# Bounding the adding write-back of a 64-expert layer to the token rows

## The chip, the cores and the metric

The kernel runs on one core of one Trainium2 chip. The metric is the time on the device of one execution, in microseconds (us). A core has five engines with instruction queues of their own (TensorE "PE", VectorE "DVE", ScalarE "ACT", GpSimd "POOL", SyncE "SP") and 16 DMA engines that move data between the on-chip memory and DRAM for all of them.

## The reference

Two transformer-like blocks in float32, one sequence of 512 tokens of width 1024. What matters here is the mixture of 64 experts at the end of the second block: each token chooses 8 experts, each expert (a gated two-layer network with hidden width 256) is applied to its tokens, and the weighted results are added up by token.

```
def routed_experts(t, top_i, top_w, w_gu, w_dn):          # t (512, 1024), top_i (512, 8)
    ...
    padded = (counts + EXPERT_BLOCK - 1) // EXPERT_BLOCK * EXPERT_BLOCK      # EXPERT_BLOCK = 128
    ...
    rows = jnp.full((P,), T, jnp.int32).at[dest].set(tok_sorted)            # empty slots name row T
    wts = jnp.zeros((P,), jnp.float32).at[dest].set(w_flat[order])
    ...
    ys = lax.map(one_block, (rows.reshape(n_blk, EXPERT_BLOCK), blk_expert)).reshape(P, D)
    out = jnp.zeros((T + 1, D), jnp.float32).at[rows].add(ys * wts[:, None])
    return out[:T]
```

512 tokens with 8 experts each are 4096 pairs of a token and an expert. Evaluating the reference's router on its inputs gives the tokens of each expert: between 1 (expert 35) and 139 (expert 36), 64 on average. 17 experts have at most 32 tokens, 19 have between 33 and 74, and 28 have 76 or more. From expert 36 to 43 all eight have 74 or more; of experts 34 to 59, nine have at most 32. Expert 63 has 101. Expert 36 is the only one with more than 128; its 11 tokens over that make up the extra block named below.

## The kernel before

The kernel is one program: a delta-rule mixer, a mixture of 32 experts, a convolution mixer, a second mixture, a sparse-attention mixer, and last the class Moe64, the stage of 64 experts that this study is about. It works through 65 blocks of CAP = 128 slots: one for each expert, and one extra block (EXTRA = 1) for the tokens that did not fit into 128 slots. A block has as many occupied slots as its expert has tokens, and its occupied slots are the first ones. So 65 x 128 = 8320 slots hold 4096 pairs, and 4224 slots are empty.

For each block there are these steps, in the methods of Moe64:

- `fetch` (four blocks ahead, AHEAD = 4) makes the lists of row numbers on VectorE: `idx` (L2431), the token of each slot, and `dst` (L2432), the row to which the slot's result goes. For an empty slot `idx` is 4096, and `dst` is 512 plus the slot's number, a spare row of its own. Then it gathers the tokens' rows from DRAM with an indirect DMA from GpSimd (L2435), which has a bound on the row number (`bounds_check=T - 1`, with T = 512) and raises no error outside of it.
- `turn` and `up` (L2448, L2458 to L2460, with the helper `parts`, L537 and L538, which splits weights into two parts on ScalarE and VectorE), `turn_hid` (L2476) and `down` (L2487 and L2489) are the matrix products of the expert. TensorE does `turn_hid` once for each block.
- `spread` (L2494) adds the 128 rows of the block's result into the DRAM tensor `sum` with an indirect DMA from GpSimd. `sum` has T + 128 = 640 rows: 512 of tokens, and 128 spare ones.

Each `spread` waits for the one before it to have landed, since both add into `sum`. The buffers of `dst` turn over six deep, so VectorE writes the `dst` of block e + 4 into the buffer that block e - 2 used, and waits for the write-back of block e - 2 to have landed. The weights (three transfers of 1 MB for each expert) come on SyncE's queue (L244) into a ring of buffers; each transfer is issued when its buffer has been used up. At the end of the loop the two last write-backs follow one another, then the 512 token rows of `sum` are loaded (L2579), normalised and written out.

Of the kernel before, what the change touches and what calls it, by code (L numbers as in the profile page):

```python
# [13 lines left out]
OP = mybir.AluOpType  # L14
# [6 lines left out]
T = 512  # L21
# [1197 lines left out]
class HierMoe:  # L1219
# [248 lines left out]
    def spread(self, oh, rows):  # L1468

        K, nc = self.K, self.nc  # L1470
        ps = K.ps(BF16)
        for i in range(4):
            nc.tensor.transpose(ps[:rows, P * i:P * i + P], oh[:, i], K.identb)
        o = K.r.rot("oht", [P, T], 2)
        nc.scalar.activation(o[:rows], ps[:rows], AF.Copy)
        return o[:rows]
# [751 lines left out]
class Moe64:  # L2228
# [263 lines left out]
    def spread(self, y, dst):  # L2492

        self.nc.gpsimd.indirect_dma_start(out=self.sum[:], out_offset=bass.IndirectOffsetOnAxis(ap=dst[:, :1], axis=0),  # L2494
                                          in_=y, in_offset=None, compute_op=OP.add)

    def run(self, xT, gain, shift, gate, last):

# [212 lines left out]
```

## Time and profile before

| | us |
|---|---|
| median of 3 runs | 3480.29 |
| lowest and highest of the runs | 3479.04 and 3489.0 |
| the profiled execution: its time | 3479.72 |
| the profiled execution: its span, first to last instruction | 3478.0 |
| TensorE busy | 3170.4 (91% of the span) |
| the expert stage, from its first write-back to the end | 2745 to 3478 |

The span leaves out 1.7 us that lie around the profiled instructions. Busy time on TensorE is modelled from pipelined matmuls, so it shows where TensorE pauses rather than how near its peak it is.

### The profile page before, as it was taken

The page shows a single profiled execution, that of the slowest core. Times are in us where ns is not written, and L with a number is a line of the kernel's source. Part 1 is how long each engine was busy: PE and PEld are TensorE (multiplying, and loading weights), DVE is VectorE, ACT ScalarE, POOL GpSimd, SP SyncE. Part 2 cuts the span into 40 slices and gives each one's busy share as a digit, 9 for nine tenths or more (in the row PEclk, how much of TensorE's full clock was granted, in tenths as well). Part 3 has the DMA queues.
Part 4 walks back from the last instruction along what each step waited for, and adds up shares of the span by engine and source line. Part 5 has one row for each costly group of instructions (what it writes and reads, how often), then busy time and mean ns, then how long its engine had stood idle before and what let it go on. Part 6 is the DMA issues. An engine that isn't in the chain of part 4 may idle for free. (4 is left out here: it accounts for less than half of the span.)

```text
span 3478.0 us, 45287 instructions
## 1 busy us (share of the span) xinstructions
PE 3170.4 (91%) x16888; PEld 1926.0 (55%) x16888; DVE 1818.4 (52%) x4124; ACT 1450.0 (42%) x2730; POOL 606.8 (17%) x687
## 2 busy tenths in 40 slices
PE   7989999888998988997999989699999899999996
PEld 4667676663333333874333333488557566666663
DVE  3567764463333334444333333565463877776675
ACT  5544763541111112332111111363454476777774
POOL 3444423300000001001000001221101122222221
PEclk9989987999999999998999999898999999999998
DMA  5211212448999996245999999212315799999996
GB/s 198 109 67 46 101 55 85 146 165 351 419 419 399 378 397 264 99 171 207 420 420 396 366 382 403 86 61 97 134 64 194 258 331 351 364 365 366 351 351 190
DMA packets 144002, 871.92 MB, mean 251 GB/s; under 512 B 26273, under 2 KB 26785, under 8 KB 49953
## 3 DMA queue, kind: packets, MB, share of 16 engines
q1 hardware_dynamic: 103824, 748.73, 53.8%
q0 software_dynamic: 35568, 109.10, 11.2%
q10 hardware_dynamic: 4384, 11.14, 0.9%
q8 instruction: 135, 2.21, 0.3%
q14 instruction: 91, 0.74, 0.1%
HBM read 844.23 MB, written 57.67 MB: 259 GB/s over the span
## 5 line engine op out<-in xcount | busy, mean ns | idle before, releaser
L1439 PE MATMUL ps<-arena 128*64 128x512 f32 x1984 | 605.8, 615 | 2.6 <-DVE arena L1484 0.3
L537 ACT ACTIVATE phase<-arena 128x512 fp32r<-128x512 f32 (+1 forms) x729 | 447.9, 618 | 356.8 <-PE ps L550 204.7
L538 DVE TENSOR_TENSOR phase<-arena,phase 128x512 fp32r<-128x512 f32 (+1 forms) x663 | 433.8, 680 | 122.6 <-ACT phase L537 118.6
L550 PE MATMUL ps<-phase 128*128 128x512 f32 (+3 forms) x1000 | 395.6, 396 | 2.8 <-POOL phase L538 2.4
L1461 PE MATMUL ps<-arena 128*64 128x512 f32 x1040 | 353.0, 617 | 33.4 <-DVE arena L1451 33.4
L1439 PEld LDWEIGHTS ps<-arena 128*64 128x64 f32 x1984 | 174.7, 142 | 297.1 <-issue 287.1
L1441 ACT ACTIVATE phase<-ps 64x512 f32<-64x512 f32 x68 | 40.0, 588 | 695.5 <-PE ps L1439 695.5
L549 PE MATMUL ps<-phase 128*128 128x512 f32 (+1 forms) x736 | 282.6, 385 | 27.1 <-DVE arena L1764 16.6
L551 PE MATMUL ps<-phase 128*128 128x512 f32 (+1 forms) x736 | 279.4, 381 | 0.9 <-POOL phase L538 0.9
L2487 PE MATMUL ps<-arena 128*128 128x512 f32 x520 | 249.8, 604 | 2.6 <-ACT arena L2478 0.8
L538 POOL TENSOR_TENSOR phase<-arena,phase 128x256 fp32r<-128x256 f32 (+1 forms) x194 | 173.7, 897 | 370.2 <-ACT phase L537 313.7
L2460 PE MATMUL ps<-phase 128*128 128x512 f32 x520 | 228.2, 439 | 0.0
L550 PEld LDWEIGHTS ps<-phase 128*128 128x128 f32 (+2 forms) x1000 | 193.4, 193 | 39.2 <-POOL phase L538 3.3
L2458 PE MATMUL ps<-phase 128*128 128x512 f32 x520 | 212.3, 408 | 2.4 <-ACT phase L537 0.5
L2459 PE MATMUL ps<-phase 128*128 128x512 f32 x520 | 206.2, 396 | 6.6 <-DVE phase L538 6.5
L1406 POOL DMA_INDIRECT phase<-hrows,phase x34 | 33.8, 995 | 952.4 <-DVE phase L1442 472.2
L1442 DVE TENSOR_TENSOR phase<-ps,phase 64x512 f32<-64x512 f32 x68 | 47.2, 695 | 289.0 <-ACT phase L1441 287.8
L1461 PEld LDWEIGHTS ps<-arena 128*64 128x64 f32 x1040 | 95.7, 139 | 174.5 <-issue 134.9
L1484 DVE SCALAR_TENSOR_TENSOR arena<-ps,arena 128x512 f32<-128x512 f32 x272 | 185.2, 745 | 11.2 <-PE ps L1483 10.1
L2494 POOL DMA_INDIRECT sum<-arena x65 | 104.5, 1607 | 489.9 <-ACT phase L537 179.8
L1465 ACT ACTIVATE phase<-ps,phase 64x512 fp32r<-64x512 f32 x136 | 92.8, 683 | 196.1 <-PE ps L1461 170.0
L549 PEld LDWEIGHTS ps<-phase 128*128 128x128 f32 x736 | 140.1, 190 | 61.4 <-issue 24.8
(630 smaller groups left out, 5710.6 us busy)
## 6 DMA issues: line engine op xcount, KB each, us to landing
arena<-in_moe SPq DMA_DIRECT2D x548, 1024.0 KB
arena<-in_ada SPq DMA_DIRECT2D x72, 1024.0 KB
phase<-in_moe SPq DMA_DIRECT2D x28, 1024.0 KB
arena<-in_wina SPq DMA_DIRECT2D x16, 1024.0 KB
arena<-in_win SPq DMA_DIRECT2D x13, 1024.0 KB
arena<-in_winb SPq DMA_DIRECT2D x12, 1024.0 KB
arena<-in_wouta SPq DMA_DIRECT2D x4, 1024.0 KB
hrows<-arena POOLq DMA_DIRECT2D x8, 512.0 KB
```

Source lines behind the costliest of these rows:

```text
L537: self.nc.scalar.activation(h, x, AF.Copy)
L538: (eng or self.nc.vector).tensor_tensor(l, x, h, op=OP.subtract)
L549: mm(ps, w[0], x[0], start=start, stop=False)
L550: mm(ps, w[0], x[1], start=False, stop=False)
L551: mm(ps, w[1], x[0], start=False, stop=stop)
L1439: nc.tensor.matmul(ph[64 * j:64 * j + 64, :], x[:, k, :], u, start=k == 0, stop=k == 7)
L1461: nc.tensor.matmul(py[64 * j:64 * j + 64, :], hT[:, k, :], u, start=k == 0, stop=k == 3)
L1484: nc.vector.scalar_tensor_tensor(xT[:, f, :], ps, gate[:, f:f + 1], xT[:, f, :], op0=OP.mult, op1=OP.add)
L2458: nc.tensor.matmul(ps, x[0], h, start=start, stop=False)
L2459: nc.tensor.matmul(ps, x[0], l, start=False, stop=False)
L2460: nc.tensor.matmul(ps, x[1], h, start=False, stop=stop)
L2487: nc.tensor.matmul(py, hid[:, P * k:P * k + P], unit[:, 1024 * k + 512 * half:1024 * k + 512 * half + 512], start=k == 0, stop=k == 1)
```

## The change

The write-back gets the bound that the gather has: rows with numbers over 511 are left out of the transfer. The lists `dst` stay as they are, so it is the empty slots that are left out. They carried zero weight and went to the spare rows, which nothing reads.

```
     def spread(self, y, dst):
 
         self.nc.gpsimd.indirect_dma_start(out=self.sum[:], out_offset=bass.IndirectOffsetOnAxis(ap=dst[:, :1], axis=0),
-                                          in_=y, in_offset=None, compute_op=OP.add)
+                                          in_=y, in_offset=None, bounds_check=T - 1, oob_is_err=False, compute_op=OP.add)
```

The order of the instructions on all five engines is the same before and after.

## Rows read from the trace of the kernel before

**Rows 1.** Busy time by stretch of the stage; (x) counts instructions, columns named above.

```profile
core 0: us, PE busy (x) PEld busy (x) DVE busy (x) ACT busy (x) POOL busy (x), PEclk, DMA share, GB/s
2745.00:3049.00 304.00, 302.50 (x1288) 200.40 (x1286) 232.93 (x506) 215.34 (x382) 72.79 (x54) 1.00 1.02 349
3122.00:3398.00 276.00, 271.13 (x1152) 176.40 (x1151) 192.67 (x449) 197.78 (x351) 78.56 (x50) 1.00 1.02 357
```

**Rows 2.** Timeline of TensorE, the transpose L2476 in four blocks: start, duration, instruction.

```profile
2939.46 0.42 PE L2476 MATMUL ps<-arena 128*128 128x128 f32 x2
...
3111.65 0.42 PE L2476 MATMUL ps<-arena 128*128 128x128 f32 x2
...
3398.49 0.42 PE L2476 MATMUL ps<-arena 128*128 128x128 f32 x2
...
3430.71 0.38 PE L2476 MATMUL ps<-arena 128*128 128x128 f32 x2
```

**Rows 3.** Waits between 3122 and 3398 us: total us, times, longest.

```profile
DVE arena L2432 <- DMA sum<-arena: 36.1, 25, 3.1
...
PEld ps L2459 <- DVE phase L538: 9.5, 21, 2.1
...
PE ps L2459 <- DVE phase L538: 3.2, 4, 1.7
```

**Rows 4.** Waits of SyncE's queue in the stage: the transfers of weights.

```profile
SPq L244 <- DVE phase L538: 563.8, 121, 8.7
```

**Rows 5.** Timeline of GpSimd: write-backs (L2494) and gathers (L2435), idle time in brackets.

```profile
2939.65 1.58 POOL L2494 DMA_INDIRECT sum<-arena  x1 [6.65 <-ACT arena L2489]
...
3116.04 1.58 POOL L2494 DMA_INDIRECT sum<-arena  x1 [8.22 <-ACT phase L537]
...
3259.72 1.86 POOL L2494 DMA_INDIRECT sum<-arena  x1 [8.24 <-ACT phase L537]
3261.89 1.55 POOL L2435 DMA_INDIRECT phase<-rows,arena  x1 [0.30 <-PE ps L2460]
...
3392.16 1.59 POOL L2494 DMA_INDIRECT sum<-arena  x1 [7.40 <-DVE arena L2432]
```

**Rows 6.** Timeline of VectorE and GpSimd around 3271 us.

```profile
3267.55 0.16 DVE L2431 SCALAR_TENSOR_TENSOR arena<-arena 128x1 int32<-128x1 f32 x1
...
3270.84 0.22 DVE L2432 SCALAR_TENSOR_TENSOR arena<-arena,phase 128x1 int32<-128x1 f32 x1 [3.13 <-DMA sum<-arena]
3270.98 4.34 DVE L538 TENSOR_TENSOR phase<-arena,phase 128x512 fp32r<-128x512 f32 x7
3271.58 1.58 POOL L2494 DMA_INDIRECT sum<-arena  x1 [8.15 <-DVE arena L2432]
```

**Rows 7.** DMA from 3100 to 3390 us: packets, MB, share of 16 engines.

```profile
q1 hardware_dynamic: 11340, 82.60, 68.4%
q0 software_dynamic: 7592, 20.98, 33.2%
...
sum<-arena POOLq DMA_INDIRECT x26
```

**Rows 8.** DMA from 2700 us to the end: packets by size, and GpSimd's queue q0.

```profile
DMA packets 46999, 253.92 MB, mean 326 GB/s; under 512 B 9440, under 2 KB 9440, under 8 KB 22880
...
q0 software_dynamic: 19152, 54.03, 31.1%
```

**Rows 9.** DMA from 2731.3 to 2732.5 us, one gather: GB/s in 40 slices, packets, queue.

```profile
GB/s 0 0 0 1 1 0 138 3 138 137 1 1 1 2 2 1 0 1 1 137 137 0 0 0 137 137 0 0 0 137 137 0 0 0 0 1 0 0 0 0
DMA packets 160, 0.04 MB, mean 31 GB/s; under 512 B 151, under 2 KB 151, under 8 KB 160
...
q0 software_dynamic: 144, 0.04, 15.9%
```

**Rows 10.** DMA from 3448.6 to 3454.8 us: the last write-back alone.

```profile
DMA  0000000000000990091658696969697979430000
...
DMA packets 144, 0.52 MB, mean 85 GB/s; under 512 B 16, under 2 KB 16, under 8 KB 144
...
q0 software_dynamic: 144, 0.52, 56.2%
```

**Rows 11.** The chain that ended last: start, us, what.

```profile
3441.74 1.55 DMA sum<-arena
3443.29 5.10 issue
...
3448.61 6.16 DMA sum<-arena
```

**Rows 12.** All gathers (L2435): durations in ns, least, median, most.

```profile
L2435 POOLq MOVE  x65: 29/29/29, 2711.2 to 3402.7; - x65
L2435 POOL DMA_INDIRECT arena<-rows,arena x44: 1011/1326/1557, 2712.3 to 3404.8; - x44
```

**Rows 13.** The indirect loads of weights (L2637), which have no bound: durations in ns.

```profile
L2637 POOL DMA_INDIRECT arena<-in_moe,phase x3: 947/972/1266, 3407.8 to 3419.5; - x3
```

## The prediction

> **What bounds the kernel now.** I read the stretches of the stage first. TensorE is busy for 302.50 of 304 us in the first part and 271.13 of 276 us in the later one, at the full clock in both, and the 16 DMA engines show a share of 1.02 in both [rows 1]. Both look full, so the question is which of them sets the pace. The timeline of TensorE answers it. From 2939.46 to 3111.65 us there are 16 blocks, so one takes 10.76 us; from 3398.49 to 3430.71, when few transfers are left, three take 10.74 each [rows 2]. That is TensorE's own pace. Between 3111.65 and 3398.49 us lie 26 blocks, 11.03 us each, which is 286.84 - 26 x 10.76 = 7.1 us more than that pace.
>
> The waits tell where the 7.1 us come from. In that stretch VectorE waits 25 times, 36.1 us in all, at L2432 for a write-back to land, and TensorE in its turn waits for VectorE's L538, which stands behind L2432 [rows 3]. One such place can be read in order of time: a write-back goes out at 3259.72 us [rows 5], L2432 waits 3.13 us and starts at 3270.84, 11.1 us after that write-back was issued; L538 starts only then, and the next write-back goes out at 3271.58, 0.74 us after the release [rows 6]. So the write-backs are a chain: each goes out when the one before it has landed. From 3116.04 to 3392.16 us it makes 25 steps of 11.04 us [rows 5], 0.28 us too slow for TensorE. It was too slow earlier as well: from 2939.65 to 3116.04 us, 16 steps took 176.39 us against TensorE's 172.19, but there the 4.2 us were only lateness, and TensorE paid nothing yet. Weights aren't the bound: SyncE waits for buffers that VectorE has not used up yet (563.8 us in all), so the weights lie ready [rows 4].
>
> Why a step takes 11 us is seen in the DMA queues. From 3100 to 3390 us the weights' queue q1 has 68.4% of 16 engines and GpSimd's queue q0 33.2% [rows 7]. Per step that is 0.684 x 11.04 = 7.6 us and 0.332 x 11.04 = 3.7 us on each DMA engine, 11.2 us together: the engines have no room left, and the write-back that shares them ends last.
>
> **What the change removes.** The order of instructions stays, so all is in the transfer itself. A gather with the same bound shows what becomes of a slot that is left out: the gather of a block with 9 tokens still has its 144 packets (128 slots and 16 ends), but only 0.04 MB [rows 9], and over the stage 54.03 MB went through q0 [rows 8], which is 8320 rows of 4 KB written back, 4096 gathered, and 3 MB of weights. So an empty slot is a tiny packet. Its price: q0 took 0.159 x 16 x 1.2 = 3.05 us of engine time there; the rows start in pairs five slices or 0.15 us apart, so nine take at least 1.35 us, and at most 1.7 us are left for 135 tiny packets, 13 ns each [rows 9].
>
> The price of an added row: q0's 20.98 MB from 3100 to 3390 us are 26 x 128 = 3328 rows written back (13.63 MB) and about 1790 gathered [rows 7]. Of 0.332 x 16 x 290 = 1540 us, the gathered rows take 1790 x 0.15 = 269 and tiny packets some 25, which leaves 1246 / 3328 = 0.37 us for a row that is added. In the last write-back, alone on the engines, it is 0.562 x 16 x 6.2 / 128 = 0.44 us [rows 10].
>
> The blocks of that stretch gather 69 rows on average (1790 / 26), so about 59 of 128 rows leave each write-back: 59 x 0.37 / 16 = 1.36 us on the mean engine for each step, some 12% of the DMA time. The chain needs 0.28.
>
> **The fullest engine** decides when a write-back lands, not the mean one. In the gather of 9 rows two engines in parallel serve four rows each and a third one serves the ninth [rows 9], so slots go to engines in runs of four. A full block has 8 rows on each engine, two runs. Where the second run begins can't be seen here. If it is at slot 64, blocks up to 64 tokens have at most four rows on an engine; if it is at slot 32, only blocks up to 32. I take the poorer, 32. Of the blocks 34 to 59, nine have at most 32 tokens. Each saves at least 4 x 0.37 = 1.5 us, together 13 us against the chain's overrun of 7.1. The longest run of full blocks, 36 to 43, overruns by 8 x 0.28 = 2.2 us even if it saves nothing, and a chain that starts the run on time has 4.2 us of lateness to spend before TensorE pays. So nearly all of the 7.1 us should come back; I take 6.5, with 0 and 7.1 as ends.
>
> The Trainium skill, "DMA: Bandwidth & Descriptors", section "The descriptor swizzle", gives the poorer answer for a transfer into 128 partitions: engine 0 serves partitions 0 to 3 and 32 to 35. It speaks against the change: half the rows is not half the landing time, and blocks of more than 35 tokens keep an engine with eight rows. By a mean over engines, the sum would be 7.1 + 1.5 us, by that rule 6.5 + 1.5; that the runs of four agree can be seen, that a write-back is split like a gather no row here shows.
>
> **The end.** The last two write-backs stand on the path that sets the end: issued at 3441.74 and at 3448.61 us, the second one landing 6.16 us later [rows 11]. The second is the extra block with 11 tokens: runs of 4, 4 and 3, so the fullest engine has 4 rows in place of 8 and it lands 4 x 0.37 = 1.5 us (up to 4 x 0.44 = 1.7) sooner. If rows went one to an engine it would be 7 x 0.44 = 3.1. The one before it (101 tokens) keeps engines with eight rows: I take 0, and at most 8 x (0.44 - 0.37) = 0.5 us. So the end gives 1.5 us, between 0 and 3.6.
>
> **What it adds.** The gathers have a MOVE of 29 ns each on GpSimd's queue, one for each [rows 12], which I take for the setting of the bound. 65 more of it are 1.9 us, hidden in GpSimd's idle time of some 7 us before each write-back [rows 5], and 0.1 us in the two last ones. The bound itself costs nothing visible: gathers with it take 1.01 to 1.56 us on GpSimd [rows 12], indirect loads without it 0.95 to 1.27 [rows 13]; if it were 0.3 us a step, the chain would have 1.08 left to gain, still enough. TensorE's pace is untouched, and once the chain is on time, it is the bound for the whole stage; nothing else is late next.
>
> **Sum.** 6.5 + 1.5 - 0.1 = 7.9 us from the profiled 3479.72: 3471.8. The median of the runs is 0.6 above the profiled time; I say 3472.
>
> **Rivals.**
> - *Tiny packets that add are not tiny.* 13 ns is the price in a gather, which writes on-chip memory. An add reads and writes DRAM for every packet. If one costs as much as a row, nothing changes in the chain or at the end: 3480. For it speaks that no row shows such a packet; against it that 4 bytes move in place of 4096.
> - *They cost more than a row*: this ends slower. A block of up to 64 tokens leaves engines with eight empty slots, and its step grows by 8 x (d - 0.37) us when d is the price of one. It decides from d = 0.37 on; at 0.42, the 33 such blocks give 33 x 0.4 = 13 us (3493), at 0.5 some 34 us (3514). The Trainium skill, same page, "Specifications", says that an engine does a read-modify-write below 512 B, which bears on this; no row here shows what it costs in an add.
> - *The fullest engine stays.* If the engines that end last are those with eight rows in most blocks, the chain remains late in the middle of the stage and about half of the 7.1 us comes back: 3.5 + 1.0 us, 3475.
> - *More than I take.* All of 7.1 and the upper end of the tail, 3.6, are 10.7 us: 3469.
>
> **How the numbers follow.** 0.3% is about what a measurement of this kernel tells from no change; against the median of 3480.29 that is 10.4 us, so faster means below 3469.9 and slower above 3490.7. My forecast (3470 to 3474) has 0.58, the fullest engine 0.15 (3474 to 3477), tiny packets as dear as rows 0.09 (3478 to 3481), dearer 0.07, more than I take 0.11. Faster by more than 0.3% are the last case and a tenth of the forecast, 0.17; slower 0.07; the rest, 0.76, within. The range from 3468 to 3480 leaves out the dearer packets, half of those as dear as rows, and the outermost part of the last case, not quite 0.2.
>
> **What would show it.** In the changed kernel's profile q0 has as many packets in the stage (19152) but 54.03 - 17.30 = 36.7 MB, and packets under 512 B rise by 4224, from 9440 to 13664. DMA share falls from 1.02 to about 0.9. L2432's wait for `sum` is gone, write-backs keep TensorE's step of 10.76 us, and 26 blocks from the 34th on take 280 us in place of 286.8. The last write-back lands in about 4.7 us in place of 6.16. I am wrong if DMA share stays or L2432 still waits with the MB gone (tiny packets are dear), or if the chain is on time and TensorE's blocks still take 11.03 us (then something else held VectorE).

## The result, and the profile after

| | before | changed |
|---|---|---|
| median of 14 runs each, us | 3483.18 | 3466.69 |
| lowest and highest, us | 3471.15 and 3496.06 | 3447.27 and 3489.51 |
| ratio, 95% interval | | 0.995 [0.9927, 0.9972] |
| profiled execution: time and span, us | 3479.72, 3478.0 | 3447.27, 3445.6 |
| its mean granted clock | 0.947 | 0.952 |

The changed kernel is faster by 0.5%. Its median lies 1.3 us below the range that was predicted (3468 to 3480) and 5.3 us below the predicted 3472.0, and the faster case, which had a chance of 0.17, is the one that came by its number; its mechanism, an end that gives up to 3.6 us, is not (the end gave 1.7).

The two profiled spans differ by 32.4 us, far more than the 16 us between the medians, so the first thing to ask is where these 32.4 us lie. The timeline of GpSimd and that of TensorE in the changed kernel give the places (start, duration, instruction).

```profile
2722.24 1.66 POOL L2494 DMA_INDIRECT sum<-arena  x1 [14.52 <-ACT arena L2489]
```

```profile
3088.27 0.42 PE L2476 MATMUL ps<-arena 128*128 128x128 f32 x2
...
3367.86 0.42 PE L2476 MATMUL ps<-arena 128*128 128x128 f32 x2
...
3399.99 0.38 PE L2476 MATMUL ps<-arena 128*128 128x128 f32 x2
```

The first write-back starts at 2722.24 us; in the profiled execution of before it starts at 2745.45. So 23.2 of the 32.4 us were gained before the first changed instruction ran, in code that is the same in both. From the first write-back to the end it takes 723.3 us in place of 732.5, and that is 9.2 us, all that the change can have done in this pair. The 26 blocks from the 34th on take 3367.86 - 3088.27 = 279.6 us in place of 286.8 [rows 2], 10.75 each, which is TensorE's own pace; the three after them take 10.71 each.

The stretches of the stage, the waits and the DMA queues stand against [rows 1], [rows 3] and [rows 7]. Busy time by stretch (columns as in that group):

```profile
core 0: us, PE busy (x) PEld busy (x) DVE busy (x) ACT busy (x) POOL busy (x), PEclk, DMA share, GB/s
2722.00:3026.00 304.00, 302.49 (x1287) 200.28 (x1285) 233.11 (x509) 215.24 (x381) 73.76 (x55) 1.00 0.94 325
3099.00:3375.00 276.00, 274.35 (x1183) 183.72 (x1182) 209.62 (x463) 203.47 (x360) 73.58 (x52) 1.00 0.96 340
```

TensorE is now busy for 274.35 of the later 276 us, where it was 271.13. The wait for `sum` at L2432 in the 26 blocks:

```profile
DVE arena L2432 <- DMA sum<-arena: 5.2, 8, 1.0
```

It was 36.1 us in 25 places; TensorE's waits at L2459 for L538 no longer stand in the list. The write-backs are still a chain, though. Block 49 (counted from 0, one for each expert) shows it: its result is ready at 3259.53 + 0.69 = 3260.22 us, and its write-back goes out at 3264.57, 4.35 us later and 0.77 us after the write-back before it has landed:

```profile
3259.53 0.69 ACT L2489 ACTIVATE arena<-ps,arena 128x512 f32<-128x512 f32 x1 [1.03 <-PE ps L2487]
...
3264.57 1.58 POOL L2494 DMA_INDIRECT sum<-arena  x1 [7.33 <-ACT phase L537]
```

Of the 25 write-backs of blocks 35 to 59, 21 go out late in this way, by up to these 4.35 us; in the kernel before all 25 do, by 4.4 to 6.5 us. TensorE pays nothing for the lateness that is left.

The DMA of the same 26 blocks, by queue:

```profile
q1 hardware_dynamic: 11306, 82.31, 75.1%
q0 software_dynamic: 7544, 14.03, 21.4%
```

GpSimd's queue fell from a third of the engines to 21.4%, but the weights' queue took 75.1% for its 82.31 MB, where it had taken 68.5% for 81.83 MB in the same 26 blocks of before (68.4% in the window of [rows 7]). Over the whole stage the packets are those that were foretold, 19152 with 36.76 MB, and 13664 under 512 B [rows 8]:

```profile
DMA packets 47001, 236.67 MB, mean 307 GB/s; under 512 B 13664, under 2 KB 13664, under 8 KB 22880
...
q0 software_dynamic: 19152, 36.76, 19.5%
```

The end, in the chain that ended last (start, us, what), against [rows 11]:

```profile
3411.03 1.55 DMA sum<-arena
3412.58 5.17 issue
...
3417.96 4.34 DMA sum<-arena
```

The last write-back lands in 4.34 us in place of 6.16, and the one before it takes as long as it did (5.17 against 5.10 us of waiting behind its issue).

### The profile page after: what moved, and what is told of

Same layout as the page of the kernel before. It is cut to its first block, busy times and chain, and to the rows that moved or that the text cites. A ratio compares the mean times of both kernels' runs of the same rounds, so it can differ in the third digit from the quotient of the medians.

```text
span 3445.6 us, 45352 instructions
## 1 busy us (share of the span) xinstructions
PE 3146.7 (91%) x16888; PEld 1910.0 (55%) x16888; DVE 1829.4 (53%) x4124; ACT 1450.6 (42%) x2730; POOL 600.5 (17%) x687
## 5 line engine op out<-in xcount | busy, mean ns | idle before, releaser
L538 DVE TENSOR_TENSOR phase<-arena,phase 128x512 fp32r<-128x512 f32 (+1 forms) x663 | 445.4, 682 | 136.6 <-ACT phase L537 132.6
L538 POOL TENSOR_TENSOR phase<-arena,phase 128x256 fp32r<-128x256 f32 (+1 forms) x194 | 176.0, 909 | 358.7 <-ACT phase L537 331.1
L2459 PE MATMUL ps<-phase 128*128 128x512 f32 x520 | 203.6, 392 | 3.3 <-DVE phase L538 3.3
L1484 DVE SCALAR_TENSOR_TENSOR arena<-ps,arena 128x512 f32<-128x512 f32 x272 | 185.2, 744 | 11.2 <-PE ps L1483 10.1
L2494 POOL DMA_INDIRECT sum<-arena x65 | 104.5, 1608 | 472.7 <-ACT arena L2489 151.3
```

What stands on the lines that cost most here:

```text
L538: (eng or self.nc.vector).tensor_tensor(l, x, h, op=OP.subtract)
L1484: nc.vector.scalar_tensor_tensor(xT[:, f, :], ps, gate[:, f:f + 1], xT[:, f, :], op0=OP.mult, op1=OP.add)
L2459: nc.tensor.matmul(ps, x[0], l, start=False, stop=False)
```

## Experiments

Two questions were open: why the median came out below the sum, and whether the reasons for the gain in the stage are the right ones. "Stage" below is the time from the first write-back to the end in the profiled execution of a kernel, 732.5 us for before and 723.3 for the changed kernel.

**1. Both kernels again (null, again).** `null` is the kernel before, `again` the changed one.

```
-    ..., bounds_check=T - 1, oob_is_err=False, compute_op=OP.add)     # changed: again
+    ..., compute_op=OP.add)                                           # before: null
```

> The kernel before, unchanged, timed against itself. If the part of the gain beyond the expert stage is chance in the granted clock ahead of the stage, two sets of runs of one and the same program differ by up to 0.2 or 0.3% here too, times go with the mean granted clock, and the stage (first write-back to end, 732.5 us before) repeats within 2 us. If runs of one program agree better than that (within 0.1%), the 16.5 us between the two medians were more than the 9 us that the stage's profile shows.

> The changed kernel once more. The change acts in the stage alone: stage 723.4 us (plus or minus 1.5) against 732.5, blocks of 10.76 us throughout, median 9 us under that of before with an uncertainty of some 5; at equal granted clock the difference is 8 to 10. If it also acts outside the stage: median 15 to 20 us under before, and still some 17 at equal granted clock.

Measured: null 3480.37 us, ratio 0.9998 [0.9975, 1.002]; again 3469.01, ratio 0.9964 [0.994, 0.9988]. The stage took 732.2 us in null and 723.7 in again. In these two pairs of profiles the stage repeats within half a microsecond, while the runs of one and the same kernel lie as far apart as 3463.79 and 3493.41 us. The 16 us of the first comparison became 13 here.

**2. Only the wait taken away (deep).** The prediction reads the write-backs as a chain closed by L2432, which waits for a buffer of `dst`. Without the bound, and with eight buffers of `dst` in place of six, that wait must vanish while the transfers stay as they were. Against before:

```
-        ..., a.rot("dst", [P, 2], AHEAD + 2).bitcast(I32)[:, 0:1]
+        ..., a.rot("dst", [P, 2], AHEAD + 4).bitcast(I32)[:, 0:1]
```

> No bound; the dst lists turn over eight deep in place of six, so VectorE never writes one whose write-back is under way. If late write-backs reach TensorE through that wait alone: L2432 waits for nothing, the 26 blocks after the 34th take 280 us (286.8 before), stage about 7 us shorter or a little less (725 to 728), while DMA share stays 1.02 and write-backs fall further behind (over 18 us after the block's transpose). If it is the DMA engines' load itself that TensorE pays for: the blocks stay at 11.0 us, with another wait in the place of this one, and the time stays.

Measured: 3488.41 us, ratio 1.0016 [0.9998, 1.0035], and the stage took 745.7 us, 13 more than before. Waits in its 26 blocks (from 3115.7 to 3402.7 us):

```profile
PEld ps L2448 <- DMA arena<-rows,arena: 8.9, 5, 3.2
```

and the stretch itself:

```profile
3115.70:3402.70 287.00, 280.02 (x1202) 186.19 (x1199) 212.59 (x467) 206.67 (x365) 70.82 (x50) 0.99 1.02 357
```

L2432 waits no more, and the blocks still take 287.0 us at a share of 1.02. That the sum is the same looks like chance, for it is made up otherwise. The transposes of blocks 34, 54 and 60 show where the time goes:

```profile
3115.68 0.42 PE L2476 MATMUL ps<-arena 128*128 128x128 f32 x2
...
3330.94 0.42 PE L2476 MATMUL ps<-arena 128*128 128x128 f32 x2
...
3402.68 0.42 PE L2476 MATMUL ps<-arena 128*128 128x128 f32 x2
```

For 20 blocks TensorE keeps its own pace of 10.76 us, as the first of the two expectations had it, while the write-backs, each still behind the landing of the one before, fall further behind their results (22 us at block 54). The last six blocks take 11.96 us each, and all waits for gathered rows but one of 0.3 us lie there. A gather stands behind a write-back in GpSimd's queue:

```profile
3340.24 1.59 POOL L2494 DMA_INDIRECT sum<-arena  x1 [9.20 <-ACT arena L2489]
3342.13 1.03 POOL L2435 DMA_INDIRECT arena<-rows,arena  x1 [0.30 <-PE ps L2448]
```

Its rows land at 3354.5 us, after the longest of TensorE's waits above, 3.2 us. So the wait at L2432 was the place where the late write-backs reached TensorE, not what made them late; two buffers more put off the payment. Behind it something new is late, the weights of the extra block (waits from 3403 to 3495 us):

```profile
ACT phase L537 <- DMA arena<-in_moe,phase: 12.6, 1, 12.6
...
PE ps L2476 <- DVE arena L2469: 10.0, 1, 10.0
```

Its indirect loads (L2637) stand in GpSimd's queue among the write-backs, and without the wait at L2432 nothing holds the write-backs' lateness down; the loads come only after them:

```profile
3425.45 0.97 POOL L2637 DMA_INDIRECT arena<-in_moe,phase  x1 [0.30 <-DVE phase L538]
3429.25 1.68 POOL L2494 DMA_INDIRECT sum<-arena  x1 [2.83 <-ACT phase L537]
3431.23 0.98 POOL L2637 DMA_INDIRECT arena<-in_moe,phase  x1 [0.30 <-issue]
```

In before the loads went out between 3407.8 and 3419.5 us [rows 13]. The six buffers had worked as a throttle.

**3. The bound, and the occupied slots spread over the engines (perm).** If the fullest engine sets the landing, a block's tokens should go one by one to different runs of four slots. The list of slot numbers does it: the first 32 tokens of a block get 32 different runs. Against the changed kernel:

```
-        nc.gpsimd.iota(self.iota, pattern=[[1, CAP]], base=0, ...)
+        nc.gpsimd.iota(self.iota, pattern=[[8, 2], [16, 2], [1, 8], [32, 4]], base=0, ...)
```

> The bound, and the occupied slots of a block spread over the 16 runs of four, so that no engine has more than one row in 16 of them. If the fullest engine decides the landing: write-backs of blocks with 40 to 75 tokens land 1 us or more sooner than in the changed kernel (about 10 us there), the step is TensorE's 10.76 nearly everywhere, and the end's last write-back lands in about 3.4 us in place of 4.34; stage 721.5 to 723 us against 723.4. If total load decides it: write-backs land after 10 us as in the changed kernel, and only the chance of the end differs.

Measured: 3467.05 us, ratio 0.9969 [0.9942, 0.9995]; stage 721.8 us, 1.6 less than the changed kernel, and the 26 blocks 279.7. The end, in its chain:

```profile
3429.24 1.55 DMA sum<-arena
3430.80 4.62 issue
...
3435.64 3.07 DMA sum<-arena
```

The last write-back lands in 3.07 us in place of 6.16, so 3.1 us sooner, which is what the prediction gave for rows that go one to an engine. In the blocks the transfers land sooner, but it brings TensorE nothing, since it was at its own pace already. What changes is that most write-backs (18 of the 25 of blocks 35 to 59) now go out when their result is ready, here 10.78 us apart (GpSimd, idle time in brackets):

```profile
3310.91 1.59 POOL L2495 DMA_INDIRECT sum<-arena  x1 [6.63 <-ACT arena L2490]
...
3321.69 1.58 POOL L2495 DMA_INDIRECT sum<-arena  x1 [6.66 <-ACT arena L2490]
```

How long the write-backs of blocks 20 to 58 took from issue to landing, by the tokens in the block, comes from the transfers' end events in the traces (means, us; one block of 33 tokens is left out):

```
tokens       before  changed  again  perm
up to 32     10.2     8.9      8.7   7.4
37 to 64     10.2    10.1     10.3   8.5
65 to 99     10.4    10.4     10.4   9.2
100 to 139   10.2    10.3     10.3  10.1
```

With the bound alone only blocks of up to 32 tokens land sooner; with the slots spread, all that are not full do.

**4. Half of the change (tail, body).** `tail` has the bound on the two last write-backs alone, `body` on all but these two. Against the changed kernel, tail (body has True and False exchanged):

```
-    def spread(self, y, dst):
+    def spread(self, y, dst, bound=False):
...
-        self.spread(*late)
-        self.spread(*finish())
+        self.spread(*late, bound=True)
+        self.spread(*finish(), bound=True)
```

> The bound on the last two write-backs alone. The chain in the middle of the stage and the end are separate terms: the 26 blocks after the 34th take 286.4 to 286.9 us as before, the last write-back lands in 4.3 us in place of 6.16, the one before it in 6.2; stage 730.3 to 731 us (1.5 to 2 under before). If the end's gain came from a chain that is on time, it stays at 6.16.

> The bound on all write-backs but the last two. The 26 blocks take 279.6 us (7.2 under before), the end is as before (6.16 us for the last one); stage 725 to 725.6 us.

Measured, a single run each: tail 3463.16 us with a stage of 733.5, body 3455.88 with 725.2. Tail's last write-back:

```profile
3433.51 4.67 DMA sum<-arena
```

From the issue of the last but one to the end tail takes 34.7 us and before 36.25, so 1.5 us are the end's. Its 26 blocks took 288.55 us, 1.7 more than before, where no difference was expected, and its stage is 2.5 us over the 731 that was expected at most; a single profile doesn't say why. The middle of tail has the code of before, so a middle can be off by 1.7 us from one profile to another. Body's 26 blocks and its last write-back:

```profile
3095.11 0.42 PE L2476 MATMUL ps<-arena 128*128 128x128 f32 x2
...
3374.89 0.42 PE L2476 MATMUL ps<-arena 128*128 128x128 f32 x2
```

```profile
3425.10 5.85 DMA sum<-arena
```

That is 279.8 us, with an end that is nearly as long as before (5.85 against 6.16 us): the two parts of the sum are separate, as the prediction had them. Both kernels' times are far below before's median with clocks of 0.952, and a single time tells nothing here.

**5. Nearly all packets tiny (none).** The bound is 0, so only rows of token 0 are added; the kernel leaves out the adding of all others. Against the changed kernel:

```
-    ..., bounds_check=T - 1, oob_is_err=False, compute_op=OP.add)
+    ..., bounds_check=0, oob_is_err=False, compute_op=OP.add)
```

> The bound at row 0, so that all rows but those of token 0 are left out (almost the whole adding is left out of the result): the price of a write-back of left-out slots. If a tiny packet costs 8 to 25 ns, the last one, alone on the engines, lands in 2.6 to 3.1 us, DMA share in the middle of the stage is 0.80 to 0.85, and the stage takes 719 to 721 us. If adding tiny packets cost as much as a row (0.37 us), it lands in about 6 us and the share stays near 1.

Measured: 3463.5 us (a single run), stage 720.1, the 26 blocks 279.8. The last write-back lands in 2.78 us, and the DMA in its window (3435.7 to 3438.5 us) shows what the 144 packets cost:

```profile
DMA packets 146, 0.03 MB, mean 9 GB/s; under 512 B 144, under 2 KB 144, under 8 KB 144
...
q0 software_dynamic: 144, 0.00, 2.5%
```

That is 0.025 x 16 x 2.8 / 144 = 8 ns for one. In the 26 blocks, where the share of the DMA engines is 0.87 and 0.80 to 0.85 was expected:

```profile
q1 hardware_dynamic: 11237, 81.78, 77.8%
q0 software_dynamic: 7488, 6.80, 8.7%
```

The middle gains no more than with the bound at 511, since TensorE is already at its pace.

**6. The gathers spread, the write-backs full (gperm).** Perm's list of slots without the bound: the load by write-backs stays, and only the gathers fall evenly on the engines. Against before it is the one line of experiment 3.

> No bound, but the occupied slots spread over the 16 runs of four, so that the gathers load all engines alike (each write-back still moves 128 rows, 8 on each engine). If the fullest engine sets the chain's step: the gather's share on it falls by up to 4 x 0.15 us, the step from 11.04 to some 10.5 to 10.8 us, write-backs are on time or nearly, the 26 blocks take 280 to 282 us and the stage 725 to 728, with the end as before (6.16 us). If the total load sets it, the share of 1.02 is the same and so are the 286.8 us and the 732.5 us.

Measured: 3471.14 us (a single run), stage 730.7, the 26 blocks 283.6 us, between what the two theories gave. The DMA of these blocks:

```profile
q1 hardware_dynamic: 11262, 82.04, 70.6%
q0 software_dynamic: 7539, 20.51, 31.3%
```

With the same MB and a mean share of still 1.02, 3.2 of the 7.2 us came back. So the mean load isn't all: how it falls on single engines counts too. It is one profile, and tail's shows that a middle can be off by 1.7 us, so the size is rough. How much of the 3.2 is due to evener engines and how much to lateness at the start of these blocks was not separated.

**7. Does the clock ahead of the stage depend on the change? (again2, none2, null2, none3).** The part of the difference that lies outside the stage went with the granted clock. Had the lighter transfers of the stage raised it, `none`, with the lightest, should do it most. again2 is the changed kernel, null2 the one before, none2 and none3 are none.

> The changed kernel, timed a third time, for the part of the gain that the stage does not show. If it is chance in the granted clock ahead of the stage: the median comes out 5 to 13 us under before this time, at equal granted clock 8 to 10 us under, and the stage takes 723.5 us again. If the change makes the rest of the program faster too: 15 us or more under once more, and the mean granted clock of its runs is higher than that of before by 0.001 or more.

> The kernel that leaves out all added rows but those of token 0, timed in rounds: if fewer transfers in the stage brought a higher granted clock elsewhere, it should show more of it than the changed kernel does (4096 rows fewer still): over 20 us under before and a granted clock above that of the changed kernel. If not, it comes out 12 to 13 us under before, which is its stage (720.1 against 732.4 us), plus or minus 5, and at equal granted clock 11 to 13.

> The kernel before again, beside the next one. Its mean granted clock stays at 0.946 to 0.947 and its median within 5 us of before; the stage takes 732.5 us.

> The kernel that leaves out all added rows but those of token 0, timed once more: its 7 runs had a mean granted clock of 0.949 against 0.946 of before, and came out 20 us under it on the mean, where its stage gives 12.6. If that was chance, the clock is 0.946 to 0.948 this time and the difference 8 to 17 us. If the clock ahead of the stage does depend on the stage's transfers, it is 0.949 again and the difference some 20 us.

Measured: again2 3470.18 us, ratio 0.9969 [0.9948, 0.999]; null2 3477.47, ratio 0.9993 [0.9972, 1.0014]; none2 3462.27, ratio 0.9943 [0.9923, 0.9964]; none3 3467.9, ratio 0.9962 [0.9939, 0.9985]. None2's runs had a mean clock of 0.9494, which spoke for such a link; none3, the same kernel, had 0.9464, and before's runs beside it 0.9461, so the link did not repeat. The nearest comparison is that of again and again2 with null and null2, 24 runs each: 0.9473 and 0.9470 against 0.9472 and 0.9470, and 8.8 us between their means (standard error 2.5), about what the stage gives. None's profiled executions have stages of 719.5 and 719.6 us, but their first write-backs at 2724.98 and 2755.37.

## Why the prediction was wrong, point by point

**The step that failed** is the last one of the sum: "The median of the runs is 0.6 above the profiled time; I say 3472", and with it "The range from 3468 to 3480", which was made of the terms of the stage alone. Both took the time ahead of the stage as known to about a microsecond, from three runs. It isn't. 100 runs of the kernel before in the experiments, its unchanged copies included, lie between 3459.6 and 3496.9 us with a standard deviation of 8.0, 38 runs of the changed one between 3447 and 3491 with 10.6. The stage repeats (732.2 to 732.5 us in three profiles of before, 723.3 to 723.7 in three of the changed), so the spread lies ahead of it, and it goes with TensorE's granted clock. Over all these runs the time falls by 3.2 us for each 0.001 of the mean clock, which leaves 2.8 us of scatter. Windows ahead of the stage show the clock itself, here the changed kernel:

```profile
0.00:700.00 700.00, 626.10 (x4668) 465.57 (x4668) 403.11 (x920) 374.83 (x799) 262.12 (x385) 0.90 0.28 100
...
2180.00:2690.00 510.00, 470.57 (x2599) 331.70 (x2600) 283.25 (x735) 241.61 (x475) 83.62 (x93) 0.97 0.29 107
```

Before has 0.88 and 0.94 there, between the levels of 0.5 (1.2 GHz) and 1 (2.4 GHz), with the same code, and again, the changed kernel once more, has 0.88 and 0.94 too. In these stretches TensorE pauses for some 8 to 11% of the time, and the granted clock differs from one execution to the next; in the stage it is busy nearly throughout and the clock stays at 1.00.

Taken over these runs, the changed kernel's mean is 3468.8 us and before's 3480.3, a gain of 11.5 with a standard error of 1.9. At equal clock it is 8.6 with a standard error of 0.5 (9.7, 6.9 and 9.1 in the three sets of the changed kernel). The forecast's 7.9 is near by this measure, and the first set of 14 runs fell 5 us further than it, most of that because its runs had on average a slightly higher clock (0.9477; the 100 runs of before have 0.9464). The remaining 3 us between 11.5 and 8.6 are, as far as the null runs and none3 show, chance in the clock; that it is only that is not shown. A miss of 1.3 us is less than this chance alone moves a median of 14 runs by, so whether it came to lie within the range or just below it was luck; that the range had no room for this chance was the mistake.

**The middle: right, a little small.** "I take 6.5", measured 7.2 (286.8 to 279.6; 279.6 and 279.7 in again and again2). All that TensorE lost came back. The reason was right: the write-backs are a chain whose step is longer than TensorE's. L2432 is only one way for its lateness to reach TensorE; with that wait gone, in deep, TensorE keeps its pace for 20 blocks and then pays through the gathers. One cost was taken too low: the run of full blocks from 36 to 43 was to cost 2.2 us of lateness and cost 3.6 (the write-back of block 36 is 0.28 us late, that of block 44 3.92). At block 49 the changed kernel is 4.35 us late, while in before, where TensorE paid, every write-back of these blocks is at least 4.4 us late. So it was a near thing that TensorE paid nothing.

**The price of an empty slot: right.** 13 ns were taken from a gather, as an upper bound, and the packet of an empty slot of a write-back takes 8 ns. So both rivals with dear packets fall. One of them rested beside a rule of the Trainium skill, "DMA: Bandwidth & Descriptors", section "Specifications", on read-modify-write below 512 B: none's last write-back, all of its packets under 512 B, lands in 2.78 us in place of 6.16, and no such cost is to be seen. Whether a slot that is left out is read and written at all, no row shows. The rest of what the bound adds was right too: each write-back now has a MOVE of 29 ns, 65 in all.

**The fullest engine: right, also for write-backs.** Blocks of up to 32 tokens land in 8.9 us in place of 10.2, those of 37 to 64 in 10.1 in place of 10.2; with the slots spread the latter land in 8.5. That a write-back is split like a gather, in runs of four that come again after 32 slots, was open; the rule of "The descriptor swizzle" on the same page of the Trainium skill agrees. The rival that the fullest engine stays was half right: the chain does remain late in the middle, but TensorE doesn't pay for it, with 26 blocks at 10.75 us.

**The end: right, a little small.** 1.5 us taken, 1.5 in tail and 1.7 in the changed kernel (36.25 to 34.5 us from the issue of the last but one to the end), 0 for the write-back of 101 tokens as taken.

**DMA share: wrong.** "DMA share falls from 1.02 to about 0.9" subtracted the rows' engine time and let the rest stay; it is 0.97 in the 26 blocks, since the same MB of weights come in less time and their packets lie longer on the engines (40.8 us of engine time for one MB in place of 38.4). GpSimd's queue did give up what was taken for the rows: 0.332 x 16 x 286.9 - 0.214 x 16 x 279.6 = 567 us, against 26 x 59 x 0.37 = 568. L2432's wait shrank to 5.2 us and did not vanish, which was named as a sign that tiny packets are dear; it isn't one here, since none shows them cheap, but a sign that the chain is still late.

## What to carry to other kernels

Ask first how far apart runs of the unchanged kernel lie and what sets that: here the time of a single run says less about a change of 9 us than the stage of one profile, which repeats within half a microsecond in six profiles of the two kernels (tail's middle, with the code of before, was 1.7 us off). A forecast of a sum from one profile needs the spread of the untouched part in its range. A wait that vanishes with an edit is not yet the cause of the loss; giving it a buffer more, with the load left as it is, tells the two apart, if it is looked at block by block: a buffer more can also put the payment off.

## What the runs showed that was not expected

- A share of DMA engines is not a load that adds up. The same 82 MB of weights took 68.5% of the engines beside full write-backs, 75.1% beside bounded ones and 77.8% with almost none. The shorter time (286.8, 279.6 and 279.8 us) explains only a part: for one MB it is 38.4, 40.8 and 42.6 us of engine time.
- After the change the write-backs run late in most of the stretch still, by up to 4.35 us, and nothing is paid for it.
- Two buffers more made the stage 13 us slower, since the wait for them had held GpSimd's queue, and the weight loads in it, on time.
- Spreading a block's tokens over the engines gave 3.2 us of 7.2 with no byte less, in one profile. With the bound as well it shortens the stage by 1.6 us more than the change, which is the shortest stage of a full computation here, though the runs' times (3467.05 and 3466.69 to 3470.18) can't tell the two apart.
